# State-space branch of a two-layer encoder: tables multiplied in place from factors turned once, and a convolution kernel stored by rows and loaded shifted

## The chip, the core and the metric

One core of a Trainium2 chip runs the whole program: TensorE (PE in the profile, with its weight loads as PEld), VectorE (DVE), ScalarE (ACT), GpSimd (POOL), the SyncE queue (SP), which issues most transfers, and 16 DMA engines between device memory and the on-chip memory. The metric is the device time of one launch in microseconds; a kernel is run several times and the median is taken. Each profile is one further execution.

## The reference, cut to what matters

The input is 1024 tokens of 1024 channels. Layer 0 projects the normalised input to `u`, gates, `q`, `k` and `v`. Its branch A, around which this change lies, is a diagonal complex state space in 64 groups of 16 channels with 64 states each:

```
bu_re = einsum('tbgh,gnh->tbgn', u_c, bb_re)     # bb = coef * b, complex
x_t   = lb * x_(t-1) + bu_t                      # lb = mag * (cos + i sin), per group and state
y     = einsum(xr, cre) - einsum(xi, cim) + dsk * u
y     = gelu(y); y = y * sigmoid(y @ glu_w + glu_b) * silu(g_s5)
```

Branch B is an eight-head chunkwise retention. One output projection joins both; layer 1 is a gated causal convolution of width 31 with a norm; every layer adds its input, and a last norm follows. All is float32 in and out.

## The kernel before, in words

**Products.** Every large product is three TensorE passes on 128x512 tiles: operands are split into a rounded part and a rest, and `mm3` (L276 to L278) adds hi*hi, hi*lo and lo*hi. One block of 128 output channels is 2 halves of 8x3 matmuls, so 48 in all. Weights come in order through `wnext`, two blocks ahead: SP loads them (`wf`), ACT rounds them (`wh`, L267), DVE or POOL makes the rest (`wl`, L268).

**The front of layer 0.** Eight blocks `u0` to `u7` make `u`, which goes to device memory (`u_d`) in a layout of 8 taps of 128 steps. DVE computes the state-space constants meanwhile (`s5_params`): powers of the multiplier for 0 to 8 steps (`pr`, `pi`), unit phases in two levels (`e1`, `e2`), and the coefficients with which POOL makes `bbr`, `bbi` (L607). Then come 16 gate blocks `g8` to `g23` (`gate_block`). With each pair of them goes one block B of the state space, 128 channels (0 to 7):

- `s5_tables(B)`, on POOL: three complex outer products of small factors (`outer`, L790 to L792; two products and one sum for the real part, the same for the imaginary part, so 18 instructions of 128x512): `Mr`, `Mi` (input side), `Tc`, `Ts` (phases), `W3` (output side). They are chained in this order, one block after another.
- `s5_states(B)`: TensorE turns `Mr`, `Mi` (8 transposes of 128x128, L837; ACT copies them to `W2`), multiplies them with `U` (L848, banks `v`). DVE turns phases, scans over the steps (L863) and turns back (L856 to L875), which gives the states `S`. Then eight small matmuls `kp` (L882, L883) with `cbr`, `cbi`, block-diagonal copies of the output coefficients from the host, give the convolution kernel of 8 taps; DVE adds the skip term (L886), TensorE turns it (L888), it is stored to `k_d`, and one load (L895) brings it back shifted into `Wd`, which ACT sorts into `W1` (L897).
- `s5_out(B)`: `y` = `W1` times `U` (L912) plus `W3` times `S` (L918), 24 products in the rows of the order, copied by ACT to `yb` and stored to `y_d`.

Beside this DVE makes sums of inputs (`input_sums`) and of output weights (`weight_sums`, L249 to L252) for later use, loaded and made in the same gate block, except the input sums of two gate blocks, which are made one block later.

**What sets the order.** A scheduler orders each engine's instructions from the program's order, priorities and its own estimate of times; `chained` and `issue_after` add order by hand. On the chip each engine and each queue runs its list in order. Aux banks are five, product banks three. Weight tiles, tables and buffers rotate by tag, so a buffer's next writer waits for its last reader.

**After the front.** Value products and retention (`mm_v`, `ktp`, `ro`), the GLU (`mm_glu`), the output projection (`mm_w`), layer 1 (`mm_a`, `mm_b`, `mm_g`, the convolution on DVE and POOL, `mm_oc`) and the final norm follow. The change does not touch them.

Of the kernel before, what the change touches and what calls it, by code (L numbers as in the profile page):

```python
# [57 lines left out]
class Trunk:  # L58
# [179 lines left out]
    def weight_sums(self, pool, k):  # L238

        nb, c = k // 2, slice(k % 2 * HALF, (k % 2 + 1) * HALF)  # L240
        v, a = self.nc.vector, []
        for q, (r, tag) in enumerate(((0, "wa"), (4, "wb"), (12, "wc"), (8, "wd"))):
            a.append(pool.tile([P, HALF], F32, name=f"a{q}_{k}", tag=tag, bufs=2))
            self.nc.sync.dma_start(a[q][:], self.A["w_out"][r + nb].rearrange("p k n -> p (k n)")[:, c])
        a11, s3, s2, s4 = (t[:] for t in a)
# [50 lines left out]
    def run(self):  # L296
# [21 lines left out]
        self.k_d = dt("k_d", [8, 112 + P, P])  # L318
# [18 lines left out]
    def layer0_front(self, st):  # L337
# [100 lines left out]
        def u_block(nb):  # L438
            ut = uv.tile([P, 8, P], F32, name=f"ut_{nb}", tag="ut", bufs=2)

            def evac(h, ps):
# [3 lines left out]
                    r.rearrange("p (m j) -> p j m", j=8), op=ALU.mult)  # L445
            if nb < 2:
                for h in range(2):
                    evac(h, u01[nb][h])
            else:
                scaled(nb, self.wnext(f"u{nb}"), f"u{nb}", evac)  # L450
            nc.sync.dma_start(self.u_d[nb].rearrange("j h g m -> (h g) j m"), ut[:])

        def gate_block(nb, w, dst):
# [8 lines left out]
            nc.sync.dma_start(dst[k * P:(k + 1) * P], gt[:])  # L462
# [3 lines left out]
        with self.tc.issue_after(xdma.ins), self.tc.issue_after(r_diag.ins):  # L466
            zero = ev.tile([P, P], F32, name="zero")
            nc.gpsimd.memset(zero[:], 0.0)
            nc.sync.dma_start(self.k_d[:, :112].rearrange("b r c -> r b c"),
                              zero[:112].unsqueeze(1).broadcast_to([112, 8, P]))  # L470
            self.s5_params(sp, ev)
        u_block(3)
        u_block(4)
        early.close()
        sums = self.pool("sums", 1, stack=st)
        self.s5 = self.pool("s5w", 1, stack=st)
        for nb in range(5, 8):
            u_block(nb)
        self.s5_tab, self.s5_back, self.s5_last = {}, {}, None
        self.s5_tables(0)  # L480
        for nb in range(8, 24):
# [15 lines left out]
            with self.tc.issue_after(self.gate_evac.ins):  # L497
                if nb in (9, 11):
                    odd = self.input_sums(sums, nb - 9)
                elif nb in (10, 12):  # L500
                    self.input_sums_made(*self.input_sums(sums, nb - 9))
                elif 13 <= nb < 21:
                    self.weight_sums(sums, nb - 13)
# [82 lines left out]
    def s5_params(self, sp, tp):  # L586
# [31 lines left out]
        self.cbr, self.cbni = load("s5_cbr", (NP, 32)), load("s5_cbi", (NP, 32))  # L618
# [3 lines left out]
        v.tensor_scalar(self.cbni[:], self.cbni[:], -1.0, None, op0=ALU.mult)  # L622
# [95 lines left out]
        self.pr, self.pi = pr_, pi_  # L718

# [24 lines left out]
        grow(e2r, e2i, 7)  # L744
        self.e1 = (e1r, e1i)
# [24 lines left out]
        self.bbr, self.bbi = t((NP, 16), keep="s5_bbr"), t((NP, 16), keep="s5_bbi")  # L770
# [3 lines left out]
        gp = nc.gpsimd  # L774
        tt(x1[0], br[:], bc(cfr), ALU.mult, gp)
# [3 lines left out]
        tt(self.bbr[:], x1[0], x1[1], ALU.subtract, gp)  # L779
        tt(self.bbi[:], x1[2], x1[3], ALU.add, gp)  # L780
# [3 lines left out]

    def outer(self, B, o_r, o_i, ar, ai, br, bi, view, op_r=ALU.subtract, op_i=ALU.add):

        gp = self.nc.gpsimd
        for o, op, (a0, b0), (a1, b1) in ((o_r, op_r, (ar, br), (ai, bi)), (o_i, op_i, (ar, bi), (ai, br))):
            t = self.big(f"o_{B}", "tmpP", 2)
            yield gp.tensor_tensor(view(t[:]), a1, b1, op=ALU.mult)  # L790
            yield gp.tensor_tensor(view(o), a0, b0, op=ALU.mult)
# [980 lines left out]
```

## Time and profile before

| what | value |
|---|---|
| three runs | 1175.82, 1178.74, 1178.51 us; median 1178.51 |
| span of the profiled execution | 1173.9 us (the page gives no other time of this execution) |
| PE / PEld / DVE / ACT / POOL busy | 1161.3 / 965.5 / 910.5 / 545.1 / 713.5 us |
| mean granted TensorE clock | 0.999 |
| moved by DMA | 270.66 MB, mean 231 GB/s |
| one pair of gate blocks with one state-space block | 29.5 us, eight of them from 97 to 333 us |

The page divides the span into 40 slices with the busy share of each engine in tenths; the views by window, by line and by time give durations and what ended each wait. "Idle before" at an engine counts only where that engine sets the end. A matmul's record overlaps the next one's, so the distance between two starts, not the record's length, is what one costs.

### The profile page before, as it was taken

To read this page: it belongs to the slowest core of one execution; us is meant where nothing else is said; L and a number is where in the kernel's file an instruction comes from. 1 tells how busy PE (TensorE), PEld (TensorE's weight loads), DVE (VectorE), ACT (ScalarE), POOL (GpSimd) and SP (SyncE) were. 2 spreads that over 40 slices of the span, in tenths; PEclk is the share of its full clock that TensorE was granted. 3 is DMA by queue.
4 is the path that set the end of the run, shared out by engine and by line. 5 is a ranking of instruction groups with operands and counts; after the bars stand their busy time and mean duration, and the time that the engine had idled before them with its cause. 6 is when DMAs were issued, how large, how long until landed. Compare 5 with 4: busy or idle time off the path is not lost.

```text
span 1173.9 us, 17492 instructions
## 1 busy us (share of the span) xinstructions
PE 1161.3 (99%) x6150; PEld 965.5 (82%) x6150; DVE 910.5 (78%) x1507; ACT 545.1 (46%) x821; POOL 713.5 (61%) x507
## 2 busy tenths in 40 slices
PE   9999999999999999999999999999999999999997
PEld 7888888888888888887788888888888888888887
DVE  7875789999717475689777888479999999999643
ACT  7212343332226642123645544367756678544662
POOL 2049999888843245664444034348894689977742
PEclk9999999999999999999999999999999999999999
DMA  9353378778789765765988468965448553357863
GB/s 344 109 178 109 134 270 312 272 269 282 273 307 325 268 228 192 251 190 180 362 313 304 160 220 268 309 232 188 161 158 306 216 182 132 134 176 243 281 247 138
DMA packets 131192, 270.66 MB, mean 231 GB/s; under 512 B 12832, under 2 KB 41760, under 8 KB 130976
## 3 DMA queue, kind: packets, MB, share of 16 engines
q1 hardware_dynamic: 129952, 265.35, 66.5%
q10 hardware_dynamic: 1152, 4.19, 0.9%
q8 instruction: 48, 0.79, 0.3%
q14 instruction: 40, 0.33, 0.1%
HBM read 193.54 MB, written 71.76 MB: 226 GB/s over the span
## 4 chain that ended last, share of the span: by engine, by line
PE 91%; DMA 4%; DVE 2%; SPq 1%; ACT 1%; POOL 1%; issue 1%; DVEq 0%; POOLq 0%; ACTq 0%
PE mm_g L277 8%; PE mm_g L278 8%; PE mm_g L276 7%; PE mm_w L278 4%; PE mm_w L277 4%; PE mm_w L276 4%; PE mm_a L278 2%; PE mm_b L277 2%; PE mm_a L276 2%; PE mm_b L278 2%; PE mm_a L277 2%; PE mm_b L276 2%; PE mm_u L278 2%; PE mm_oc L278 2%; PE mm_u L277 2%; PE mm_oc L277 2%
## 5 line engine op out<-in xcount | busy, mean ns | idle before, releaser
L1461 DVE SCALAR_TENSOR_TENSOR cv<-u,convw,cv 128x512 f32<-128x512 f32 x358 | 244.7, 750 | 5.0 <-ACT cv L1447 3.5
L1441 POOL TENSOR_TENSOR tp<-tp,tp 128x512 f32<-128x512 f32 x104 | 138.9, 1338 | 28.7 <-ACT tp L1440 23.4
L278 PE MATMUL mm_g<-xh,wl_g 128*128 128x512 f32 x256 | 100.8, 394 | 0.0
L277 PE MATMUL mm_g<-xl,wh_g 128*128 128x512 f32 x256 | 100.7, 394 | 0.0
L276 PE MATMUL mm_g<-xh,wh_g 128*128 128x512 f32 x256 | 100.5, 393 | 0.0
L1440 ACT ACTIVATE tp<-u,convw 128x512 f32<-128x512 f32 x104 | 69.6, 713 | 9.6 <-POOL tp L1441 9.4
L277 PEld LDWEIGHTS mm_g<-xl,wh_g 128*128 128x128 f32 x256 | 48.1, 188 | 11.2 <-issue 1.6
L278 PEld LDWEIGHTS mm_g<-xh,wl_g 128*128 128x128 f32 x256 | 48.0, 188 | 10.5
L276 PEld LDWEIGHTS mm_g<-xh,wh_g 128*128 128x128 f32 x256 | 48.1, 188 | 9.6
L278 PE MATMUL mm_oc<-zh,wl_woc 128*128 128x512 f32 (+1 forms) x152 | 54.5, 360 | 0.2 <-DMA wl_woc<-lo_woc 0.2
L276 PE MATMUL mm_oc<-zh,wh_woc 128*128 128x512 f32 (+1 forms) x152 | 54.3, 362 | 0.0
L277 PE MATMUL mm_oc<-zl,wh_woc 128*128 128x512 f32 (+1 forms) x152 | 54.0, 357 | 0.0
L276 PE MATMUL mm_glu<-yh,wh_glu 128*128 128x512 f32 x128 | 50.0, 392 | 1.3 <-ACT sg L1250 1.3
L277 PE MATMUL mm_u<-xl,wh_u 128*128 128x512 f32 x128 | 50.1, 391 | 1.0 <-DVE xl L390 0.9
L276 PE MATMUL mm_g<-h1h,wh_cg 128*128 128x512 f32 x128 | 50.3, 393 | 0.0
L276 PE MATMUL mm_a<-h1h,wh_ca 128*128 128x512 f32 x128 | 50.3, 393 | 0.0
L278 PE MATMUL mm_b<-h1h,wl_cb 128*128 128x512 f32 x128 | 50.3, 393 | 0.0
L232 ACT CAST lh<-lf 128x512 fp32r<-128x512 f32 x32 | 19.5, 618 | 65.9 <-DMA lf<-w_c 59.3
L278 PE MATMUL mm_a<-h1h,wl_ca 128*128 128x512 f32 x128 | 50.0, 391 | 0.0
L277 PE MATMUL mm_glu<-yl,wh_glu 128*128 128x512 f32 x128 | 50.0, 392 | 0.0
L278 PE MATMUL mm_g<-h1h,wl_cg 128*128 128x512 f32 x128 | 49.9, 390 | 0.0
L277 PE MATMUL mm_g<-h1l,wh_cg 128*128 128x512 f32 x128 | 49.9, 390 | 0.0
(811 smaller groups left out, 3637.3 us busy)
## 6 DMA issues: line engine op xcount, KB each, us to landing
wf_g<-w_ab SPq DMA_DIRECT2D x16, 512.0 KB, 5.4
a<-w_out SPq DMA_DIRECT2D x32, 256.0 KB, 4.4
ws<-a SPq DMA_DIRECT2D x32, 256.0 KB, 4.8
lf<-w_c SPq DMA_DIRECT2D x32, 256.0 KB, 5.3
wf_p<-ws SPq DMA_DIRECT2D x16, 512.0 KB, 4.1
wf_cb<-w_c SPq DMA_DIRECT2D x16, 512.0 KB, 4.9
wf_ca<-w_c SPq DMA_DIRECT2D x16, 512.0 KB, 4.7
wl_cb<-lo_cb SPq DMA_DIRECT2D x16, 512.0 KB, 3.4
```

Of the source, the lines that this page charges most:

```text
L232: self.nc.scalar.copy(hi[:], f[:])
L276: nc.tensor.matmul(ps, wh[:, kb, :], xh, start=start, stop=False)
L277: nc.tensor.matmul(ps, wh[:, kb, :], xl, start=False, stop=False)
L278: self.last_mm = nc.tensor.matmul(ps, wl[:, kb, :], xh, start=False, stop=stop)
L1440: nc.scalar.mul(sk[:], u[:, k:k + HALF], cw[:, nb, k:k + 1])
L1441: gp.tensor_tensor(s0[:], s0[:], sk[:], op=ALU.add)
L1461: v.scalar_tensor_tensor(dst[:], *tap, accs_[i][:], op0=ALU.mult, op1=ALU.add)
```

## The change

- **Input tables.** The factors are turned once: after the first half of `u6`, TensorE transposes `pr`, `pi` (4) and `bbr`, `bbi` (8), ACT copies the three banks and stores them to device memory (`pt_d`, `bt_d`). For each block four loads (`PT`, `BT`, real and imaginary) bring the factors already repeated over rows, and POOL multiplies them in place (`outer`, 6 plain instructions of 128x512) into the turned table itself. The 8 transposes and 2 copies of each block are gone. Block 0's loads are on ACT's queue, the others on SP's, and these tables have one buffer each.
- **Phase and output tables.** `outer3` makes a complex product with three real products and two sums (5 instructions in place of 6) from precomputed sums (`psum`, `csum`, `cdif`, `e1s`, `e2s`, and `e1i - e1r` in place of `e1i`). A block thus has 16 POOL instructions in place of 18. `W3` has nine taps, of which the first is a copy of the output coefficients by ACT.
- **Convolution kernel.** `kp` is made from `W3` and block-diagonal copies of `bbr`, `bbi` made on the chip by ACT (the host's `cbr`, `cbi` and their two loads of 512 KB are gone); four small products with the identity add the skip term. The result is stored by rows of 112+128 and loaded by eight shifted loads straight into `W1`: the transpose, the DVE sum, the copy `Kt` and ACT's sorting copy are gone. The zeros of `k_d` are now 112 columns in place of 112 rows.
- **Times and queues.** `s5_kernel(B+1)` is called one gate block ahead of its states; `s5_states(B)` comes after the first gate block of its pair in place of before it. Input and weight sums are loaded one gate block before they are made. The stores of gates and of `y` move from SP's to ACT's queue. `U` is loaded with the tables. `R8`, `tmpP` and `tmpV` have fewer buffers.

The diff, cut:

```diff
@@ u_block
+                if (nb, h) == (6, 0):
+                    with tc.issue_after(self.last_mm.ins):
+                        self.s5_turned(ev)
@@ gate_block
-            nc.sync.dma_start(dst[k * P:(k + 1) * P], gt[:])
+            nc.scalar.dma_start(dst[k * P:(k + 1) * P], gt[:])
@@ layer0_front
         for nb in range(8, 24):
             B = (nb - 8) // 2
+            gate_block(nb, self.wnext(f"g{nb}"), self.gs_d if nb < 16 else self.gr_d)
             if nb % 2 == 0:
+                if B:
+                    self.s5_out(B - 1)
+                if B < 2:
+                    self.s5_kernel(B)
                 self.s5_states(B)
-                if nb in (10, 12):
-                    with self.tc.issue_after(self.last_kg.ins):
-                        self.input_sums_made(*odd)
-            gate_block(nb, self.wnext(f"g{nb}"), self.gs_d if nb < 16 else self.gr_d)
-            if nb % 2 == 0 and B:
-                self.s5_out(B - 1)
-            if nb % 2 and B < 7:
-                self.s5_tables(B + 1)
+                if B < 7:
+                    self.s5_tables(B + 1)
+            elif 0 < B < 7:
+                self.s5_kernel(B + 1)
...
+    def s5_turned(self, tp):
...
+            for i, src in enumerate(srcs):
+                nc.tensor.transpose(ps[:, i * P:(i + 1) * P], src, self.ident[:])
+            t = tp.tile([P, 8, P], F32, name=f"turned_{name}", tag="xin", bufs=8)[:, :4, :]
+            self.last_turn = nc.scalar.copy(t.rearrange("p i n -> p (i n)"), ps[:])
+            n = len(srcs) // len(dsts)
+            for i, dst in enumerate(dsts):
+                nc.scalar.dma_start(dst.rearrange("(i p) n -> p i n", p=P), t[:, i * n:(i + 1) * n, :])
...
+        for blk, b in zip(self.bblk, (self.bbr, self.bbi)):
+            for g in range(2):
+                r = slice(64 * g, 64 * g + 64)
+                with self.tc.issue_after(self.last_turn.ins):
+                    nc.scalar.copy(blk[r, :, 16 * g:16 * g + 16], b[r].rearrange("p h q -> p q h"))
...
+    def outer(self, B, ar, ai, br, bi):
+
         gp = self.nc.gpsimd
...
+        t = self.big(f"o_{B}", "tmpP", 1)
+        for o, a, b, op in ((t, ai, bi, ALU.mult), (ai, ai, br, ALU.mult), (br, ar, br, ALU.mult), (br, br, t, ALU.subtract),
+                            (ar, ar, bi, ALU.mult), (ar, ar, ai, ALU.add)):
+            yield gp.tensor_tensor(o[:], a[:], b[:], op=op)
+
+    def outer3(self, B, o_r, o_i, k1, k2, k3, view, op_i):
...
@@ s5_tables
+        queue = nc.sync if B else nc.scalar
+        self.chained(queue.dma_start(t[:], bass.AP(tensor=d.tensor, offset=d.offset + qs.start * P, ap=ap))
+                     for t, d, ap in zip((PT[0], BT[0], PT[1], BT[1]), (self.pt_d[0], self.bt_d[0], self.pt_d[1], self.bt_d[1]),
+                                         ([[32 * P, 8], [0, 16], [1, 4 * P]], [[0, 8], [32 * P, 16], [1, 4 * P]]) * 2))
...
+        order = (inputs, outputs, turns) if B == 0 else (outputs, inputs, turns) if B == 1 else (outputs, turns, inputs)
+        self.s5_last = self.chained(chain(*order), self.s5_last)
@@ s5_states
-            for q in range(4):
-                nc.tensor.transpose(ps[:, q * P:(q + 1) * P], M[:, q, :], self.ident[:])
-            t = self.big(f"W2{nm}_{B}", f"W2{nm}", 1)
-            nc.scalar.copy(t[:].rearrange("p q n -> p (q n)"), ps[:])
...
-        nc.tensor.transpose(kp[:, :P], Kg[:], self.ident[:])
...
+    def s5_kernel(self, B):
...
+        made += [nc.tensor.matmul(kp[r, :P], self.bblk[0][:, q0 + q, :], W3[:, 0, q, :P], start=True, stop=False)
+                 for q, r in enumerate(rows)]
+        made += [nc.tensor.matmul(kp[r, :16], self.ident[:, r], self.dd[:, B, :], start=False, stop=False) for r in rows]
+        made += [nc.tensor.matmul(kp[r, :P], self.bblk[1][:, q0 + q, :], W3[:, 1, q, :P], start=False, stop=True)
+                 for q, r in enumerate(rows)]
+        self.chained(made)
+        Kg = self.s5.tile([P, P], F32, name=f"Kg_{B}", tag="Kg", bufs=1)
+        copied = nc.scalar.copy(Kg[:], kp[:, :P])
+        nc.scalar.dma_start(self.k_d[B, :, 112:], Kg[:])
...
+        for g in range(8):
+            nc.sync.dma_start(W1[:, g, :], bass.AP(tensor=kd.tensor, offset=kd.offset + g * 16 * n,
+                                                   ap=[[16, 8], [n, 16], [1, P]]))
```

**TensorE around block 0.** Names: `mm_u7`, `mm_g8`, `mm_g9` are products of those blocks, `turn_*` the new transposes. Before, the transposes stand between `u7` and `g8`, and states and `kp` late in the first half of `g8`:

```order
L277 MATMUL mm_u7_1_1010<-xl_7_1_219,wh_u7_859 128x512
L278 MATMUL mm_u7_1_1010<-xh_7_1_218,wl_u7_860 128x512
L837 MATMUL w2r_0_1073<-ident_69,Mr_0_1037 128x128 x4
L837 MATMUL w2i_0_1080<-ident_69,Mi_0_1038 128x128 x4
L276 MATMUL mm_g8_0_1153<-xh_0_0_134,wh_g8_919 128x512
```

Now the twelve transposes stand in the middle of `u6`, and `kp` and the states of block 0 stand in the middle of the first half of `g9`, twelve matmuls after its start:

```order
L282 MATMUL mm_u6_0_927<-xh_7_0_214,wl_u6_803 128x512
L810 MATMUL turn_p_957<-ident_69,s5_pr_574 128x128 x2
L810 MATMUL turn_p_957<-ident_69,s5_pi_575 128x128 x2
L810 MATMUL turn_br_966<-ident_69,s5_bbr_728 128x128 x4
L810 MATMUL turn_bi_974<-ident_69,s5_bbi_729 128x128 x4
L280 MATMUL mm_u6_1_986<-xh_0_1_142,wh_u6_802 128x512
```

```order
L282 MATMUL mm_g9_0_1293<-xh_3_0_174,wl_g9_1023 128x512
L941 MATMUL kp_0_1176<-W3_0_1092,s5_bblkr_474 32x128 x4
L943 MATMUL kp_0_1176<-s5_s5_dd_478,ident_69 32x16 x4
L944 MATMUL kp_0_1176<-W3_0_1092,s5_bblki_475 32x128 x4
L903 MATMUL v0_0_1206<-U_0_1086,PTr_0_1082 64x128 x8
L903 MATMUL v1_0_1215<-U_0_1086,BTr_0_1084 64x128 x8
L280 MATMUL mm_g9_0_1293<-xh_4_0_184,wh_g9_1022 128x512
```

The states of block 0 have moved back by about one and a quarter gate blocks, and they no longer wait for transposes of their own. From block 2 on `kp` stands between the blocks of a pair and `y` and `v` side by side after the pair's first block.

**ScalarE's queue at the turned factors.** Nothing of this stood there before. `ptr`, `pti`, `btr`, `bti` are the tensors in device memory, `PTr_0` to `BTi_0` block 0's tables:

```order
L812 COPY turned_br_971<-turn_br_966 128x512
L815 DMA ptr_953<-turned_p_962 128x2x128
L815 DMA pti_954<-turned_p_962 128x2x128
L815 DMA btr_955<-turned_br_971 128x4x128
L812 COPY turned_bi_979<-turn_bi_974 128x512
L827 COPY s5_bblkr_474<-s5_bbr_728 64x32x16 x2
L827 COPY s5_bblki_475<-s5_bbi_729 64x32x16 x2
L815 DMA bti_956<-turned_bi_979 128x4x128
L871 DMA PTr_0_1082<-ptr_953 128x1x512
L271 CAST wh_g9_1022<-wf_g9_1021 128x1024
L871 DMA BTr_0_1084<-btr_955 128x1x512
L871 DMA PTi_0_1083<-pti_954 128x1x512
```

`BTi_0` comes next. The store of `bti` stands behind four copies, and the loads behind that store. **POOL's chain** continues from there; before, `Mr` followed `bbi` directly:

```order
L615 TENSOR_TENSOR s5_bbi_729<-s5bb1_731 128x32x16
L838 TENSOR_TENSOR o_0_1095<-BTi_0_1085,PTi_0_1083 128x512
L838 TENSOR_TENSOR BTi_0_1085<-BTi_0_1085,PTr_0_1082 128x512
L838 TENSOR_TENSOR PTr_0_1082<-BTr_0_1084,PTr_0_1082 128x512
L838 TENSOR_TENSOR PTr_0_1082<-PTr_0_1082,o_0_1095 128x512
L838 TENSOR_TENSOR BTr_0_1084<-BTr_0_1084,PTi_0_1083 128x512
L838 TENSOR_TENSOR BTr_0_1084<-BTr_0_1084,BTi_0_1085 128x512
L844 TENSOR_TENSOR o_0_1102<-s5_psum_610,s5_s5_cr_470 128x512
```

The first of these waits for the loads of `BTi_0` and `PTi_0`.

More of the change, by code (lines that the diff above doesn't have):

```diff
@@ L473, in layer0_front @@
         u_block(4)
+        for nb in (5, 6):
+            u_block(nb)
         early.close()
@@ L854, in s5_states @@
         vr, vi = V[0][:], V[1][:]
-        t2, t4 = (fl(self.big(f"m{i}_{B}", "tmpV", 4)) for i in range(2))
+        t2, t4 = (fl(self.big(f"m{i}_{B}", "tmpV", 2)) for i in range(2))
         v.tensor_tensor(t2, vi, ts, op=ALU.mult)
@@ L874, in s5_states @@
         v.tensor_tensor(c1(S[:, 0]), c0(zr), c0(t2), op=ALU.subtract)
-        v.tensor_tensor(c1(S[:, 1]), c0(zi), c0(t3), op=ALU.add)
+        self.last_s = v.tensor_tensor(c1(S[:, 1]), c0(zi), c0(t3), op=ALU.add)
         v.memset(S[:].rearrange("p c q m -> p (c q) m")[:, :, 0:1], 0.0)
-        kp = self.bank(f"kp_{B}")
-        for q in range(4):
-            o = kp[q * 32:(q + 1) * 32, :P]
-            nc.tensor.matmul(o, self.cbr[:, q0 + q, :], Mr[:, q, :], start=True, stop=False)
-            nc.tensor.matmul(o, self.cbni[:, q0 + q, :], Mi[:, q, :], start=False, stop=True)
@@ L894, in s5_states @@
-        kd = self.k_d[B]
-        nc.sync.dma_start(Wd[:], bass.AP(tensor=kd.tensor, offset=kd.offset, ap=[[P, P], [16 * P, 8], [1, P]]))
-        W1 = w.tile([P, 8, P], F32, name=f"W1_{B}", tag="W1", bufs=2)
-        nc.scalar.copy(W1[:].rearrange("p g (i h) -> p i g h", i=8), Wd[:].rearrange("p i (g h) -> p i g h", g=8))
-        self.s5_back[B] = U, W1, W3, S
+        self.s5_state[B] = S
+    def s5_kernel(self, B):
+        nc, W3 = self.nc, self.s5_tab[B][2]
+        q0 = 4 * B
+        kp, made = self.bank(f"kp_{B}"), []
+        rows = [slice(q * 32, (q + 1) * 32) for q in range(4)]
+        made += [nc.tensor.matmul(kp[r, :P], self.bblk[0][:, q0 + q, :], W3[:, 0, q, :P], start=True, stop=False)
[7 more added lines that the diff above has]
+        nc.scalar.dma_start(self.k_d[B, :, 112:], Kg[:])
+        R8 = self.s5_r8[B] = self.big(f"R8_{B}", "R8", 1)
+        with self.tc.issue_after(copied.ins):
+            for q in range(4):
+                nc.scalar.mul(R8[:, q, :], self.m01[:], self.r8[:, 4 * B + q:4 * B + q + 1])
+        W1 = self.s5.tile([P, 8, P], F32, name=f"W1_{B}", tag="W1", bufs=2)
+        kd, n = self.k_d[B], 112 + P
+        for g in range(8):
+            nc.sync.dma_start(W1[:, g, :], bass.AP(tensor=kd.tensor, offset=kd.offset + g * 16 * n,
+                                                   ap=[[16, 8], [n, 16], [1, P]]))
+        self.s5_w1[B] = W1
@@ L1739, in layout @@
     A["s5_cr"], A["s5_ci"] = c(inp["s5_c_re"][0]), c(inp["s5_c_im"][0])
-    for k in ("r", "i"):
-        cc = A["s5_c" + k].reshape(2, 64, 32, 16)
-        z = np.zeros((2, 64, 32, 2, 16), f)
-        for g in range(2):
-            z[g, :, :, g, :] = cc[g]
-        A["s5_cb" + k] = z.reshape(P, 32, 32)
     dd = np.zeros((8, 8, 16, 16), f)
```

124 lines of the change are left out of this document (68 added, 56 removed).

## The prediction

> **What bounds the kernel now.** I read the page's busy table and chain first, then what TensorE waited for, then the gate blocks by windows.
>
> ```profile
> span 1173.9 us, 17492 instructions
> PE 1161.3 (99%) x6150; PEld 965.5 (82%) x6150; DVE 910.5 (78%) x1507; ACT 545.1 (46%) x821; POOL 713.5 (61%) x507
> PE 91%; DMA 4%; DVE 2%; SPq 1%; ACT 1%; POOL 1%; issue 1%; DVEq 0%; POOLq 0%; ACTq 0%
> PE mm_glu L276 <- ACT sg L1250: 1.3, 1, 1.3
> PE mm_oc L278 <- DMA wl_woc<-lo_woc: 0.2, 1, 0.2
> ```
>
> The first three rows are the page's, the other two are the longest and the last wait of TensorE over the whole span: outside the head and the tail it is never idle for longer than 1.3 us. The chain follows it for 91%. So a pass taken from TensorE is worth its time, wherever it stands, as long as no other engine comes late; a pass added costs the same.
>
> ```profile
> 126.61:156.11 29.50, 29.50 (x203) 24.69 (x202) 24.14 (x29) 9.94 (x18) 27.68 (x20) 1.00 0.55 196
> 185.62:215.12 29.50, 29.50 (x203) 24.69 (x202) 28.14 (x32) 9.92 (x19) 27.33 (x20) 1.00 0.86 301
> 274.14:303.64 29.50, 29.50 (x203) 24.68 (x202) 27.36 (x30) 8.03 (x14) 25.74 (x19) 1.00 0.80 276
> ```
>
> These are windows of one pair of gate blocks each: length, then PE, PEld, DVE, ACT and POOL busy, granted clock, DMA share, GB/s. PE fills each window at full clock. But DVE (24.1 to 28.1) and POOL (25.7 to 27.7) are nearly full as well; the slack of the two is the second thing that decides.
>
> **The change part by part.** First TensorE's prices, from its instructions in order of time (start, length):
>
> ```profile
> 90.02 0.39 PE L276 MATMUL mm_u<-xh,wh_u 128*128 128x512 f32 x1
> 99.99 0.39 PE L278 MATMUL mm_u<-xh,wl_u 128*128 128x512 f32 x1
> 100.67 0.39 PE L278 MATMUL mm_u<-xh,wl_u 128*128 128x512 f32 x1
> 102.01 0.40 PE L277 MATMUL mm_g<-xl,wh_g 128*128 128x512 f32 x1
> 106.58 0.39 PE L276 MATMUL mm_g<-xh,wh_g 128*128 128x512 f32 x1
> 109.73 0.39 PE L278 MATMUL mm_g<-xh,wl_g 128*128 128x512 f32 x1
> 115.65 0.39 PE L277 MATMUL mm_g<-xl,wh_g 128*128 128x512 f32 x1
> 116.22 0.40 PE L276 MATMUL mm_g<-xh,wh_g 128*128 128x512 f32 x1
> ```
>
> From 90.02 to 99.99 there are 44 matmuls: 0.2266 us each. From 100.67 to 102.01 stand two steps of this and the 8 transposes: 1.34 - 0.45 = 0.88, so 0.11 a transpose. From 106.58 to 109.73 stand two steps, `v` and `kp`: 2.70. From 115.65 to 116.22 two steps and the transpose of `Kg`: 0.12. The merged chain gives the rest (start, time):
>
> ```profile
> 156.11 0.44 PE w2r L837 x4
> 156.55 0.44 PE w2i L837 x4
> 162.01 1.90 PE v L848 x32
> 171.19 1.79 PE y L912 x16
> 172.98 1.99 PE y L918 x32
> ```
>
> So `v` is 1.90, `y` 3.78, and `kp` with what it costs to turn aside is 2.70 - 1.90 = 0.80, in 16 passes on quarters of the array; without some 0.25 for the turn these are 0.55, or 0.034 a pass.
>
> *Removed*: 9 transposes in each of 8 blocks, 8 x (0.88 + 0.12) = 8.0 us. *Added once*: 12 transposes at 0.11 and one more turn aside of 0.1: 1.4. *Added per block*: four small products with the identity, 8 passes of 16 columns. No row has these. At `kp`'s price they are 8 x 0.034 = 0.27; at that of a full pass of `y` (1.79 / 16 = 0.112) 0.9; and the new order, which takes all four quarters one after another, may give `kp` back 0.1, so below nothing down to -0.1. I take 0.2, next to `kp`, since they stand on the same quarters: 1.6 for eight blocks, between -0.8 and 7.2. TensorE's sum is -8.0 + 1.4 + 1.6 = **-5.0**; a pair shrinks from 29.5 to some 28.7.
>
> The rest costs nothing if it stays hidden. Two groups of it by line:
>
> ```profile
> L897 ACT COPY W<-Wd 128x1024 f32<-128x1024 f32 x8 | 8.4, 1052 | 47.2 <-DMA Wd<-k_d 47.2
> L886 DVE TENSOR_TENSOR Kg<-Kg,s_s_dd 128x16 f32<-128x16 f32 x8 | 5.7, 714 | 0.0
> ```
>
> ACT, at 8 to 10 of 29.5 us a pair, gives up two copies of 0.58, `Kt` and the 1.05 of `W1`, and takes two small copies and store issues. DVE gives up 0.7 for the skip term: its 27.4 becomes 26.7 in 28.7. DMA moves four more loads of 256 KB a pair: 276 GB/s in 29.5 us is 8.1 MB, so 9.2 MB in 28.7, 320 GB/s, where 301 took a share of 0.86; so 0.91, full but not over. SP had 24 transfers in a pair and gets 31 (it loses `k_d`, `Wd`, `y_d`, two gate stores; it gains 4 + 8). Its loads for block B+1 wait for block B's `v`, because these tables have one buffer, and behind them wait loads of `w_out`, which DVE sums 16 us or more later; the weights behind them are two blocks (22 us) ahead. What is late in the states is DVE's, and `S` is needed by `y` a whole pair later than `v`.
>
> **The one place where it may show is the first blocks.** Block 0's tables used to follow `bbi` on POOL. Now they wait for a round trip.
>
> ```profile
> 38.80 0.69 DVE L622 TENSOR_SCALAR s_s_cbi<-s_s_cbi 128x1024 f32<-128x1024 f32 x1
> 67.95 0.44 DVE L607 TENSOR_TENSOR s_e1r<-s5t,s5t 128x256 f32<-128x256 f32 x1
> 81.64 1.29 POOL L607 TENSOR_TENSOR s_bbi<-s5bb 128x512 f32<-128x512 f32 x1
> L839 ACT COPY W2r<-w2r 128x512 f32<-128x512 f32 x8 | 4.6, 579 | 0.0
> L934 ACTq DMA_DIRECT2D yn_d<-yn x8: 326/362/389, 364.7 to 417.6; - x8
> xa<-xT SPq DMA_DIRECT2D x8, 256.0 KB, 5.3
> outT<-fo SPq DMA_DIRECT2D x8, 256.0 KB, 2.2
> x<-xT SPq DMA_DIRECT2D x7, 512.0 KB, 8.9
> ```
>
> DVE gets sums of 288, 544 and 544 columns ahead of the coefficients, by the 0.44 of 256 columns some 1.9, and loses 0.69: `bbi`, done at 82.9, is done near 84.1. TensorE reaches the middle of `u6` at 100.90 - 72 x 0.2266 = 84.6 and asks for `bbi` at 85.4: no wait, with 1.3 to spare. The banks are turned at 85.9. ACT then has, after two copies, three stores (0.36 each), a copy and four copies of half the lanes (0.58 each): the store of `bti` is issued near 90.9. It lands, and three issues later (1.1) the last load starts and lands. A transfer of 256 KB took 5.3 in just this stretch (the row of `xa`, windowed at 74 to 110 us), 2.2 in an empty one: POOL starts between 90.9 + 2.2 + 1.1 + 2.2 = 96.4 and 102.6. `U`, `u_d` and eight `xa` fill the queue here, so I take **100.5**, near the upper end.
>
> ```profile
> 108.00 1.11 POOL L790 TENSOR_TENSOR o<-s_bbi,s_pi 128x512 f32<-128x512 f32 x1
> 132.75 1.11 POOL L790 TENSOR_TENSOR o<-s_bbi,s_pi 128x512 f32<-128x512 f32 x1
> 160.46 2.09 POOL L790 TENSOR_TENSOR o<-s_bbi,s_pi 128x512 f32<-128x512 f32 x1
> ```
>
> These rows each start a block's 18 instructions: 24.75 us, or 1.375 an instruction, while DVE was lightly loaded, then 27.71, or 1.54. TensorE asks for `kp_0` at 100.90 + 1.4 + 60 x 0.2266 = 115.9, for which POOL must have made 11 instructions; for `kp_2` (37) at 115.9 + 2.8 + 84 x 0.2266 + 6.6 + 10.9 = 155.2; for `v_2` (48) at 155.2 + 0.9 + 10.9 + 3.8 = 170.8. POOL, with 22 at 1.375 and the others at 1.54, is there at 115.6, 153.9 and 170.8: just in time three times. Later it gains, 16 x 1.5 = 24 us of work in 28.7. So a start between 96.4 and 102.6 costs TensorE 0 to 2.1 us once; I take 0.7.
>
> ```profile
> 85.14 1.22 DVE L268 TENSOR_TENSOR wl_g<-wf_g,wh_g 128x1024 fp32r<-128x1024 f32 x1 [4.67 <-ACT wh_g L267]
> 85.26 2.26 POOL L792 TENSOR_TENSOR Mr<-Mr,o 128x512 f32<-128x512 f32 x1
> 89.73 1.30 POOL L792 TENSOR_TENSOR Mi<-Mi,o 128x512 f32<-128x512 f32 x1
> ```
>
> A POOL instruction that starts just behind a DVE one with two inputs lasts 2.26 instead of 1.30. The Trainium skill, page "SBUF — State Buffer", section "Who interferes with whom", says why: a VectorE instruction with two inputs in SBUF and a GpSimd one that reads SBUF exclude each other for their whole length. By that rule alone, POOL's instructions could never overlap DVE's sums and low halves, and the first blocks would pay those in full; the trace agrees in these three rows, and this is the first rival's mechanism.
>
> **The sum.** -5.0 + 0.7 = -4.3. The span would be 1169.6; the median of the runs shown stands 4.6 above the profiled span, which I take as what lies around it, so the forecast is 1178.5 - 4.3 = **1174.2**. That nothing behind the front gives it back follows from TensorE having no wait there that another engine's clock time sets; the 1.3 us at `mm_glu` hangs on products of retention, which move along.
>
> **The rivals.** *POOL paces the first blocks.* If the 1.54 holds from the start, `v_2` waits until 100.5 + 48 x 1.54 = 174.4, with the later start 176.5: a stall of 3.6 to 5.7, and the time is 1177.1 to 1179.2, no change. For it speak the two rows of 1.375 and 1.54 and the windows with POOL at 27.7; against it that DVE has nothing to do for block 0 until its tables are there. *The round trip is slow* (the slower side). The store of `bti` and the load behind it may take what loads took at the queue's fullest, 8.9 each: POOL starts at 90.9 + 8.9 + 1.1 + 8.9 = 109.8, 9.3 later, and all of it lands on TensorE at `kp_0` and `v_2`: 1178.5 - 5.0 + 9.3 = 1182.8. It makes the kernel slower than the uncertainty from a start at 109 on. Against it stands 5.3 as the landing time in this stretch. *The kernel does not give what it says*: if the identity products cost full passes, 7.2 instead of 1.6, TensorE gains nothing and the time is 1179.8 with the same 0.7. Against it stand `kp`'s 0.034. *DVE paces the pairs*: it decides only if DVE needs over 28.7 a pair, and its fullest window, 28.1 less 0.7, does not; at 30 us it would cost six pairs 1.3 each, 1182.
>
> ```profile
> k_d<-zero SPq DMA_DIRECT2D x1, 448.0 KB, 10.1
> ```
>
> One more rule speaks against a detail. The Trainium skill, page "DMA: Bandwidth & Descriptors", section "Specifications", gives 512 bytes as the smallest transfer at full rate; the zeros of `k_d` now go in rows of 448 bytes in the full queue of the head. By the rule that store lasts longer than its 10.1 us in the trace, and can hold up `x`; no row of before shows rows below 512 bytes by themselves.
>
> **How the numbers follow.** Chances: forecast 0.56, POOL pacing 0.17, slow round trip 0.12, full-price products 0.10, DVE 0.05. The forecast's own range, from the ends of its two unknown terms taken half way, is 1171 to 1177; the range over all takes in the first and third rival: 1171 to 1180.5. A measurement of this kernel can tell about 0.3%, 3.5 us, from no change. The forecast lies 4.3 below, only 0.8 beyond that bound, so of its 0.56 some 0.45 counts as faster, and the lower ends of the rivals add 0.08; slower are the slow round trip, DVE and a part of the full-price products: 0.15; the rest, 0.32, is no change.
>
> **What would show it.** Right: windows of a pair of 28.5 to 28.8 us from block 3 on with PE full; no transposes but twelve; TensorE idle once at most, under 2 us, before `kp_0`, `kp_2` or `v_2`, released by POOL. Wrong: a POOL instruction on `BTi` that starts after 103; waits of TensorE for POOL in several blocks or for banks held by DVE; the identity products longer than 0.4 us a block; pairs that do not shrink.

## The result, and the profile after

The changed kernel takes 1209.03 us (median of four runs, 1208.46 to 1212.94) against 1177.72 us before (four runs, 1175.82 to 1178.74): a ratio of 1.0276, 95% interval 1.0258 to 1.0295. It is slower by some 31 us. The forecast was 1174.2, the range ended at 1180.5, so both missed. One execution further down, of the kernel with only the order 16 x 8, ran at a mean granted clock of 0.556 and took 1946.37 us; its time is left out there, and the profile of that kernel is of this execution.

The profiled execution has a span of 1206.4 us, 32.5 more than before. The page, with the same rows that opened the prediction (span, busy time, shares of the chain by engine):

```profile
span 1206.4 us, 17642 instructions
PE 1166.9 (97%) x6154; PEld 967.5 (80%) x6154; DVE 906.4 (75%) x1502; ACT 534.9 (44%) x812; POOL 698.5 (58%) x495
PE 74%; DMA 13%; DVE 5%; POOL 4%; issue 2%; ACT 1%; SPq 1%; ACTq 0%; DVEq 0%; POOLq 0%
```

TensorE is still the busiest engine, but it holds 74% of the chain where it held 91, and transfers hold 13% where they held 4. What it waited for, the five longest over the whole span (total, times, longest):

```profile
PE v L903 <- POOL PTr L838: 10.3, 3, 7.2
PE v L903 <- POOL BTr L838: 8.4, 5, 2.4
PE kp L944 <- POOL W L848: 2.7, 2, 1.9
PE kp L941 <- POOL W L846: 1.8, 1, 1.8
PE mm_v L1123 <- ACT wh_V L166: 1.9, 1, 1.9
```

Before, no wait between the head and the tail was longer than 1.3 us. Now the products `v` and `kp` wait for POOL's tables, 23.2 us in all, and in most blocks, not once. POOL in turn waited for this, between 80 and 400 us:

```profile
POOL o L838 <- DMA BTi<-bti: 43.7, 6, 13.0
POOL o L838 <- DMA xa<-xT: 18.9, 1, 18.9
POOL o L838 <- DMA ws<-a: 9.9, 1, 9.9
```

`o` is the first product of a block's input tables, and it needs the loads of the turned factors. All eight of its waits end with a transfer (two are put down to other transfers that came last there, `xa` and `ws`): by this view POOL is not too slow, it has nothing to work on. Five of the pairs, from the start of one block's `y` to that of the next (length, then PE, PEld, DVE, ACT, POOL busy, granted clock, DMA share, GB/s):

```profile
174.86:204.92 30.06, 29.14 (x202) 23.97 (x201) 26.86 (x32) 7.67 (x17) 20.81 (x14) 1.00 0.89 286
204.92:245.96 41.04, 32.48 (x201) 26.65 (x200) 24.55 (x29) 7.12 (x16) 28.01 (x21) 0.83 0.82 273
245.96:274.48 28.52, 28.52 (x201) 23.84 (x200) 23.20 (x29) 7.12 (x16) 18.20 (x13) 1.00 0.89 290
274.48:308.89 34.41, 30.30 (x202) 25.03 (x200) 23.78 (x29) 7.13 (x16) 23.95 (x18) 0.95 0.82 271
308.89:341.60 32.71, 30.32 (x201) 24.96 (x200) 20.60 (x24) 7.13 (x16) 22.80 (x17) 0.95 0.80 258
```

One pair has no wait: 28.52 us with PE full, where a pair took 29.50. So TensorE's saving is there, 0.98 a pair. The other four give it back many times over: 1.5, 12.5, 5.9 and 4.2 us above 28.52. About two thirds of that is waiting; most of the rest is the clock, as the lowered means of the granted clock in three of the rows show. TensorE's instructions around the longest wait (start, length):

```profile
216.05 1.98 PE L903 MATMUL v<-U,PTr 128*64 128x128 f32 x16 [7.20 <-POOL PTr L838]
219.39 1.97 PE L903 MATMUL v<-U,BTr 128*64 128x128 f32 x16 [1.37 <-POOL BTr L838]
222.31 0.63 PE L282 MATMUL mm_g<-xh,wl_g 128*128 128x512 f32 x1
222.74 0.63 PE L280 MATMUL mm_g<-xh,wh_g 128*128 128x512 f32 x1
225.59 0.39 PE L281 MATMUL mm_g<-xl,wh_g 128*128 128x512 f32 x1
225.82 0.40 PE L282 MATMUL mm_g<-xh,wl_g 128*128 128x512 f32 x1
```

After 8.6 us of waiting the matmuls start 0.43 us apart until 225.3 and then again 0.23: windows of one microsecond there show a granted clock of 0.50. The pair's 12.5 us are 8.6 of wait and some 4 of half clock.

The loop that this forms is seen whole at block 7. Block 6's `v` is over at 317.3. SP's queue, what the loads stand behind, and the loads (start, length of the issue):

```profile
319.49 0.48 SPq L874 DMA_DIRECT2D U<-u_d  x1
320.71 1.43 SPq L258 DMA_DIRECT2D ws<-a  x2
324.46 0.84 SPq L258 DMA_DIRECT2D ws<-a  x1
325.41 0.60 SPq L871 DMA_DIRECT2D PTr<-ptr  x1
328.28 0.57 SPq L871 DMA_DIRECT2D BTi<-bti  x1
```

and POOL's first and last instruction on them, and TensorE's second half of `v`:

```profile
339.22 1.29 POOL L838 TENSOR_TENSOR o<-BTi,PTi 128x512 f32<-128x512 f32 x1 [9.20 <-DMA BTi<-bti]
348.06 1.26 POOL L838 TENSOR_TENSOR BTr<-BTr,BTi 128x512 f32<-128x512 f32 x1
349.38 1.09 PE L903 MATMUL v<-U,BTr 128*64 128x128 f32 x16 [1.47 <-POOL BTr L838]
```

From `v` to the first load's issue 8.1 us, to the last issue 2.9, to its landing 10.9, POOL's six instructions 10.1: 32 us from `v` to `v`, against 28.52 of work for TensorE.

### The profile page after: what moved, and what is told of

It is laid out like the page before. It is cut to its first block, busy times and chain, and to the rows that moved or that the text cites. A ratio compares the mean times of both kernels' runs of the same rounds, so it can differ in the third digit from the quotient of the medians.

```text
span 1206.4 us, 17642 instructions
## 1 busy us (share of the span) xinstructions
PE 1166.9 (97%) x6154; PEld 967.5 (80%) x6154; DVE 906.4 (75%) x1502; ACT 534.9 (44%) x812; POOL 698.5 (58%) x495
## 4 chain that ended last, share of the span: by engine, by line
PE 74%; DMA 13%; DVE 5%; POOL 4%; issue 2%; ACT 1%; SPq 1%; ACTq 0%; DVEq 0%; POOLq 0%
PE mm_g L280 5%; PE mm_g L281 4%; PE mm_g L282 4%; PE mm_w L280 4%; PE mm_w L282 4%; PE mm_w L281 4%; PE mm_oc L280 2%; PE mm_oc L282 2%; PE mm_a L282 2%; PE mm_oc L281 2%; PE mm_b L282 2%; PE mm_b L281 2%; PE mm_a L280 2%; PE mm_a L281 2%; PE mm_b L280 2%; PE mm_glu L280 2%
## 5 line engine op out<-in xcount | busy, mean ns | idle before, releaser
L280 PE MATMUL mm_g<-xh,wh_g 128*128 128x512 f32 x256 | 103.3, 403 | 0.0
L1501 ACT ACTIVATE tp<-u,convw 128x512 f32<-128x512 f32 x104 | 69.7, 714 | 11.1 <-POOL tp L1502 10.9
L466 ACT ACTIVATE gt<-gt 128x512 f32<-128x512 f32 x32 | 20.2, 632 | 107.0 <-DVE gt L465 78.8
L465 DVE TENSOR_TENSOR gt<-mm_g,R 128x512 f32<-128x512 f32 x32 | 21.8, 684 | 43.4 <-PE mm_g L282 43.4
L838 POOL TENSOR_TENSOR o<-BTi,PTi 128x512 f32<-128x512 f32 x8 | 10.3, 1284 | 72.4 <-DMA BTi<-bti 43.7
```

The lines of the kernel that those rows point to most:

```text
L280: nc.tensor.matmul(ps, wh[:, kb, :], xh, start=start, stop=False)
L465: self.gate_evac = nc.vector.tensor_tensor(gt[:, c], ps[:], self.R[:, c], op=ALU.mult)
L466: nc.scalar.activation(gt[:, c], gt[:, c], AF.Silu)
L838: yield gp.tensor_tensor(o[:], a[:], b[:], op=op)
L1501: nc.scalar.mul(sk[:], u[:, k:k + HALF], cw[:, nb, k:k + 1])
```

## The experiments

All ratios are to the kernel before on the same chip. Where no interval is given, a kernel was run once. The kernels that were run several times spread over up to 10 us when their loads come late (1182.67 to 1192.32 for one below), so a few us between two single runs say nothing.

### Leave the loads out

```diff
+        if B == 0:
+            self.s5_pt, self.s5_bt = (... one set of four tables ...)
+        PT, BT = self.s5_pt, self.s5_bt
+        if B == 0:
             self.chained(queue.dma_start(t[:], ...) ...)
```

> The changed kernel without the four loads of the turned factors for blocks 1 to 7: POOL multiplies again what block 0 left in the same four tables, so the state inputs of these blocks are left out (wrong numbers, same instructions on TensorE, DVE, ACT and POOL). Theory A (a loop through one buffer: states of block B-1 free the tables, the loads come 6 to 11 us later in SP's queue, land 11 to 13 us after their issue, POOL needs 8 to 10 us, then states of block B; 32 us and more against 28.5 us of TensorE work a pair): TensorE's waits for POOL before the states of blocks 3 and 5 to 7 (8.6 and 9.2 us) go, with the slow clock behind them; the wait of block 0 (3.7 us) stays; 1178 to 1184 us, pairs of 28.5 us. Theory B (POOL's own rate beside DVE, 16 instructions at 1.6 to 2.1 us): the waits stay within 30%, over 1195 us.

This kernel leaves out the state inputs of blocks 1 to 7. It takes 1176.88 us, against 1178.13 before. All waits for input tables were gone; what was left were the two at block 0's `kp`, 4.1 us together:

```profile
PE kp L944 <- POOL W L846: 2.2, 1, 2.2
PE kp L947 <- POOL W L848: 1.9, 1, 1.9
```

Theory B (POOL too slow beside DVE) falls: POOL does the same instructions here. The cause is with the loads. The time lies 1.1 us below the range, in a single run.

### Two buffers, and block 0's order

```diff
-        PT, BT = ([self.big(f"{n}{c}_{B}", n + c, 1) for c in "ri"] for n in ("PT", "BT"))
+        PT, BT = ([self.big(f"{n}{c}_{B}", n + c, 2 if c == "r" else 1) for c in "ri"] for n in ("PT", "BT"))
```

> The changed kernel with two buffers for the two tables that the states read (real parts), so that no load of block B+1 waits for the states of block B, and the loads stand up to a pair earlier in SP's queue; the same bytes are moved. Theory A (the loop through one buffer): as without the loads, 1178 to 1186 us, POOL's wait for the loads under 10 us in blocks 2 to 7 together. Theory B (POOL's rate): over 1195 us. Theory C (the transfers are too many: 1 MB more a pair in queues that are full): still over 1195 us, with POOL waiting for the loads as before (44 us), while the kernel without these loads is fast.

```diff
-        order = (inputs, outputs, turns) if B == 0 else (outputs, inputs, turns) if B == 1 else ...
+        order = (outputs, inputs, turns) if B == 1 else (outputs, turns, inputs)
```

> The changed kernel with one edit: block 0's output and phase tables are made ahead of its input tables, so POOL works on them while the round trip through device memory runs. Only the first stall is touched. Theory A: the wait of 3.7 us before kp and states of block 0 and its slow clock (some 2 us) go, the waits of blocks 3 to 7 stay: 1202 to 1206 us. If the later waits only take up what the first one leaves (they are set by a fixed point in time, as transfers in a full queue would be): 1207 to 1211 us.

> Both edits together: two buffers for the real tables, and block 0's output and phase tables first. Theory A: TensorE has no wait over 1 us in the gate blocks, and the sum of the prediction stands alone: 8 pairs 0.98 us shorter, 1.4 us of transposes, so 1177.7 - 6.5 = 1171 to 1176 us. Theories B and C: over 1190 us.

Two buffers: 1206.22 us, ratio 1.0237 (1.0222 to 1.0252). Block 0's order: 1205.04, 1.0235 (1.0218 to 1.0252). Both: 1196.36, 1.0156 (1.0141 to 1.0171). Theory A in its plain form (1178 to 1186 with two buffers, 1171 to 1176 with both) falls with the first and the third. The buffers did take away the waits of `v` for POOL, but the time did not go with them. What TensorE waited for with two buffers:

```profile
PE mm_v L1123 <- ACT wh_V L166: 12.6, 1, 12.6
PE kp L941 <- POOL W L846: 5.2, 1, 5.2
PE mm_g L280 <- DVE gt L465: 3.2, 3, 2.5
```

The same lateness comes out elsewhere, the largest piece 12.6 us behind the front, at the value products, whose weights ScalarE rounds late (`wh_V`). That speaks for the loop through one buffer as the place where the lateness showed and not as its source; the next kernel tests it. The order of block 0 is worth some 4 us by itself, as expected, and 10 on top of two buffers (1206.2 to 1196.4).

### The same loads from plain rows

```diff
+        if B:
+            src = [self.A["w_out"][2 * B + i // 2] ... 128 rows of 512 columns ... for i in range(4)]
+        self.chained(queue.dma_start(t[:], s) for t, s in zip((PT[0], BT[0], PT[1], BT[1]), src))
```

> The changed kernel with the four table loads of blocks 1 to 7 on the same queue, at the same places and of the same size, but from 128 different rows of a weight tensor in place of 8 or 16 rows repeated (so the state inputs of these blocks are left out: wrong numbers). Theory C1 (loads that repeat rows of device memory are slow in themselves; in a quiet stretch 1 MB of them and 0.5 MB of kernel rows kept the transfer engines only 0.45 busy): under 1190 us, with POOL's waits for the loads at half (44 to some 20 us) and landings near 5 us. Theory C2 (it is the loads' place and number: SP's list in order, the bytes in a full stretch, the one buffer): 1200 to 1212 us, as the change.

1185.69 us, again without the state inputs of blocks 1 to 7. Same queue, same places, same bytes, one buffer, block 0's order as in the change: some 23 of the 31 us are gone. POOL's waits for these loads were halved:

```profile
POOL o L838 <- DMA BTi<-w_out: 23.1, 6, 6.9
```

So it is neither the bytes nor the place alone: a load of the turned factors is slow in itself. That is C1, within its numbers for the time and for POOL's waits. The kernel changes three things of a load at once: its groups, the repetition, and the tensor that it reads (`w_out` in place of `pt_d` and `bt_d`, which the kernel itself writes).

### What makes such a load slow

The loads of the change read 8 groups of 16 rows, of which only 8 or 16 differ. Two kernels part the grouping from the repetition:

```diff
+        src: ... w_out ...          ap=[[P * D, 8], [D, 16], [1, 4 * P]]   # 8 groups of 16 different rows
+        src: ... pt_d and bt_d ...  ap=[[0, P], [1, 4 * P]]                # one row, 128 times
```

> The changed kernel with the table loads of blocks 1 to 7 from 128 different rows of a weight tensor, but written as 8 groups of 16 rows, as the loads of the change are (state inputs of these blocks left out). It parts two readings of the 1185.7 us of the kernel with plain rows. If a load slows because rows are repeated: as with plain rows, 1183 to 1189 us, two loads back to back in the quiet stretch after block 0's states at 340 to 360 GB/s. If it slows because its outer dimension is 8, so that only half of the transfer engines take part: 1203 to 1212 us, and in that stretch at most 185 GB/s with the engines 0.45 to 0.5 busy, as in the change.

> The other corner: the table loads of blocks 1 to 7 all read one row 128 times, as one group of 128 (state inputs of these blocks are wrong). If repeating rows is what slows: 1203 to 1215 us. If the outer dimension of 8 does: 1183 to 1189 us, and the rate of the two loads in the quiet stretch at 300 GB/s or above.

8 groups of different rows: 1199.18 us, between the two ranges. One row 128 times: 1209.99. Both leave out the state inputs of blocks 1 to 7. Neither reading was right alone: by these single runs each of the two costs. After block 0's states two table loads, 0.5 MB, are for some us the only transfers under way, but for the end of the loads of `W` before them. Windows of one microsecond there (the last two columns are the share of the transfer engines and GB/s), the change first:

```profile
133.00:134.00 1.00, 1.00 (x6) 0.84 (x5) 1.00 (x2) 0.22 (x1) 0.92 (x2) 1.00 0.50 184
134.00:135.00 1.00, 1.00 (x6) 0.81 (x6) 1.00 (x1) 0.84 (x1) 0.61 (x1) 1.00 0.32 119
135.00:136.00 1.00, 1.00 (x6) 0.84 (x5) 0.96 (x3) 0.00 (x0) 0.00 (x0) 1.00 0.49 170
```

then plain rows:

```profile
134.00:135.00 1.00, 1.00 (x7) 0.81 (x6) 1.00 (x2) 0.05 (x1) 0.77 (x1) 1.00 0.85 257
135.00:136.00 1.00, 1.00 (x6) 0.84 (x5) 0.96 (x3) 1.00 (x1) 0.00 (x0) 1.00 0.71 266
```

then 8 groups of different rows:

```profile
136.00:137.00 1.00, 1.00 (x6) 0.84 (x5) 1.00 (x3) 0.00 (x0) 0.00 (x0) 1.00 0.49 182
137.00:138.00 1.00, 1.00 (x6) 0.84 (x5) 1.00 (x3) 0.00 (x0) 0.00 (x0) 1.00 0.51 158
```

and one row 128 times:

```profile
135.00:136.00 1.00, 1.00 (x6) 0.84 (x5) 0.96 (x2) 0.81 (x1) 0.22 (x1) 1.00 0.65 162
136.00:137.00 1.00, 1.00 (x6) 0.84 (x5) 1.00 (x3) 0.25 (x1) 0.00 (x0) 1.00 0.88 152
```

The two windows of plain rows hold 523 KB, which is both loads: 2 us. The change needs more than 3 for the same bytes. With 8 groups, different rows or not, the share is never above 0.51 and the rate never above 184 GB/s, as if the load used half of the engines. With one row 128 times the engines are busier, and the rate in the windows shown is 152 and 162 all the same: reading a row again and again is slow in another way. Plain rows reach 257 and 266 in the same place.

The two kernels with repeated rows read tensors that the kernel writes itself, the two with different rows read `w_out`. That this is not the difference shows far behind, in the profile of the change: two loads of 256 KB with 128 different rows, `gl` and `x1l`, come from such tensors with nothing else under way, and 522 KB are moved in 2 us:

```profile
1082.00:1083.00 1.00, 1.00 (x6) 0.81 (x6) 1.00 (x3) 0.00 (x0) 0.00 (x0) 1.00 0.80 303
1083.00:1084.00 1.00, 1.00 (x6) 0.84 (x5) 1.00 (x3) 0.85 (x1) 0.44 (x1) 1.00 0.57 219
```

### The order 16 x 8

The tables' 128 rows are 8 taps x 16 channels. Putting them as 16 channels x 8 taps, with `U` and the shifted loads to match, gives all these loads 16 groups; the repetition stays.

```diff
-  [[32 * P, 8], [0, 16], [1, 4 * P]], [[0, 8], [32 * P, 16], [1, 4 * P]]
+  [[0, 16], [32 * P, 8], [1, 4 * P]], [[32 * P, 16], [0, 8], [1, 4 * P]]
-  self.u_d[B].rearrange("j h g m -> (j h) g m")
+  self.u_d[B].rearrange("j h g m -> h j (g m)")
-  ap=[[16, 8], [n, 16], [1, P]]
+  ap=[[n, 16], [16, 8], [1, P]]
```

> The changed kernel, with the 128 rows of the tables in the order 16 channels x 8 taps in place of 8 taps x 16 channels, in three access patterns (the table loads, the load of U, the eight shifted loads of the convolution kernel): the same values, bytes and number of transfers, and each of these loads now has an outer dimension of 16. The rows are still repeated. If the outer dimension of 8 is a main part of the cause in the change itself: two table loads in the quiet stretch after block 0's states at 300 GB/s or more, POOL's waits for the loads cut to half, and the time 1185 to 1197 us. If only repeating rows counts: 1205 to 1212 us.

> The same, with block 0's output and phase tables ahead of its input tables. By the same reading the first stall goes too: 4 to 6 us below the kernel with the order 16 x 8 alone; 1180 to 1192 us.

> The same as the one before, with two buffers for the real tables (loads on SP's queue). If what is left after the order 16 x 8 is the loop through one buffer: 1174 to 1180 us. If it is the transfers: within 3 us of the kernel with one buffer.

Alone 1207.96 us (1204.56 to 1208.61), ratio 1.0241 (1.0219 to 1.0264); with block 0's order 1199.55, 1.0182 (1.0155 to 1.0209); with two buffers as well 1193.58, 1.0123 (1.0100 to 1.0147). All three lie above the ranges in which the 8 groups, or the one buffer after them, would be a main part of the cause. The grouping by itself buys nothing: the kernel with 16 groups of repeated rows is where the change is. Its windows with the two table loads alone, 516 KB in 3 us:

```profile
202.00:203.00 1.00, 1.00 (x4) 0.50 (x3) 0.96 (x2) 0.00 (x0) 0.00 (x0) 0.56 0.52 176
203.00:204.00 1.00, 1.00 (x4) 0.61 (x3) 1.00 (x3) 0.00 (x0) 0.00 (x0) 0.56 0.56 176
204.00:205.00 1.00, 1.00 (x4) 0.50 (x3) 0.95 (x2) 0.00 (x0) 0.00 (x0) 0.56 0.54 164
```

The share is a little above a half, and the rate, 164 to 176, is no higher than with 8 groups: it seems that now the repetition sets it. The two limits are close, 184 GB/s at most for 8 groups and 152 to 176 for repeated rows, and lifting one of them leaves the other. Beside other edits the order does buy something: 5.5 us with block 0's order (1199.55 against 1205.04) and 6.1 with the loads on ScalarE's queue (below), in both cases with intervals of the ratio that do not touch.

### The loads on ScalarE's queue

> Two buffers for the real tables, block 0's other tables first, and all table loads on ScalarE's queue in place of SP's; the same bytes. If the loads' place in SP's list is the cause (they come 6 to 12 us behind the time at which their tables are free, and what stands behind them waits for their issue): TensorE's waits of this kernel with the loads on SP (9.1 us before the value products, 6.2 us before kp, 2.0 for DVE) shrink to a third and the time is 1174 to 1182 us. If it is the transfers themselves (bytes, repeated rows): 1190 to 1200 us, as with the loads on SP (1196).

> The kernel with two buffers, block 0's other tables first and the table loads on ScalarE's queue (1188.6 us), with plain rows in place of the repeated ones (state inputs of blocks 1 to 7 left out). If nothing is left but the rate of the loads: within 3 us of the kernel without loads and with the same order (1173.8), so 1173 to 1177 us. If their bytes cost as well, through the value weights that come late: 1180 to 1188 us.

> Order 16 x 8, two buffers, block 0's other tables first, and the table loads on ScalarE's queue: the kernel of 1188.6 us with all its loads spread over twice the engines. With plain rows it took 1176.8. If the rate of the loads was all that kept it above: 1174 to 1180 us, faster than or equal to before; if repeating rows costs by itself: 1182 to 1188 us.

> The kernel of 1182.5 us (order 16 x 8, two buffers, block 0's other tables first, table loads on ScalarE's queue) with one more edit: the loads of y for its pass through gelu go on ScalarE's queue too. Its one long wait of TensorE, 10.9 us before the value products, hangs on ScalarE's gelu, which waits for that load behind the value phase's loads in SP's list. If that place in the list is the cause: the wait shrinks to under 2 us and the time is 1169 to 1175 us, below the kernel before. If the transfers of this stretch are simply too many: the wait moves to the next load, 1179 to 1185 us.

With two buffers, block 0's order and the table loads moved by `queue = nc.scalar`: 1188.60 us, 1.0089 (1.0061 to 1.0117). That is 8 us below the same kernel with the loads on SP (1196.36), outside both ranges that I gave: the place in SP's list counts, but it is not all. With plain rows in addition, which leaves out the state inputs of blocks 1 to 7: 1176.79. With the order 16 x 8: 1182.51, 1.0041 (1.0026 to 1.0057), the fastest version with all its loads. TensorE's waits in its gate blocks are gone but for one of 1.6 us for DVE; what is left stands at the value products:

```profile
PE mm_v L1123 <- ACT wh_V L166: 10.9, 1, 10.9
```

I took that for a place in SP's list and moved the loads of `y` to ScalarE's queue (`nc.sync` to `nc.scalar` in `y_pass`). It was wrong: 1185.76, 1.0067 (1.0045 to 1.0089), and the wait is still 9.1 us. The profiles show what stands ahead of the late rounding in ScalarE's list: casts of `xf` and a gelu of `yp`. In the version at 1182.51 ScalarE waits 19.7 us for the first `xf`, until 365.3, and the gelu then follows `yp` at 373.1; after the move the gelu waits 8.8 us for `yp`, issued at 355.5, until 367.9. Why these loads come late is not shown. With plain rows the wait for `wh_V` was 0.6, so they seem late through what the slow loads leave behind.

### Old input tables in the new kernel, and no loads at all

```diff
+        M, W2 = W2, []
+        for nm, m in zip("ri", M):
+            for q in range(4):
+                nc.tensor.transpose(ps[:, q * P:(q + 1) * P], m[:, q, :], self.ident[:])
```

> The changed kernel with the input tables made as before: POOL multiplies the unturned factors, TensorE turns both tables of each block (8 transposes, 0.88 us a block), ACT copies them; the twelve transposes, the stores and the loads of the turned factors are gone. The convolution kernel by rows, the new order, the queues and the earlier loads of sums stay. If the loads of the turned factors are the whole cause: no stall, TensorE's work is the new pair of 28.5 plus 0.88, so 29.4, against 29.5: 1174 to 1179 us, no difference from before. If the rest of the change costs too: over 1182 us.

> Without the loads for blocks 1 to 7 (state inputs of these blocks left out, as in the first of these kernels) and with block 0's other tables first. If the prediction's sum for TensorE is right by itself, both stalls being gone: the 1176.9 us of the kernel without loads less the 4.1 us that TensorE waited there before kp and the 1 to 2 us of slow clock behind it: 1170 to 1173 us. If something else in the change costs (the eight shifted loads, stores on ScalarE's queue): 1175 to 1179 us.

> The kernel without the loads of blocks 1 to 7 and with block 0's other tables first (state inputs of these blocks left out), timed in rounds this time: what TensorE's sum is worth with no stall. One look gave 1173.8 us against 1178.2, so a ratio of 0.9963; if TensorE's sum of the prediction holds (-5.0 us), 1172 to 1175 us and the ratio's interval below 0.998.

Old input tables, everything else new: 1180.30 us, ratio 1.0014 (1.0001 to 1.0026), some 2 us above before and just above the range, with pairs of 29.58 us (`y` starts at 201.41 and 230.99). So the kernel by rows, the queues and the earlier loads of sums cost 2 or 3 us at most. Without the loads of blocks 1 to 7, and so without their state inputs, and with block 0's order: 1173.82 in a single run, and 1171.16 as the median of five (1170.55 to 1178.73), ratio 0.9942 (0.9926 to 0.9959). Two pairs of the single run:

```profile
137.92:166.44 28.52, 28.52 (x223) 23.75 (x222) 25.73 (x29) 11.35 (x24) 25.02 (x17) 1.00 0.78 257
166.44:194.96 28.52, 28.52 (x202) 23.84 (x201) 27.91 (x32) 7.00 (x15) 23.75 (x17) 1.00 0.87 295
```

That is TensorE's saving with nothing late: 6 to 7 us. It is what the change could have been worth if these loads had cost nothing. No version that keeps all its loads is below the kernel before.

## Why the prediction was wrong

- **TensorE's sum, -5.0.** Right in kind and a little small. 8 pairs x 0.98 = 7.8, less 1.4 for the twelve transposes and 0.5 for a wait at `turn_bi`, is -5.9; the kernel without the loads has -6.0 by its medians. The four products with the identity were the term that was furthest off: `kp` with them runs from 148.56 to 149.20 in the change, 0.64 where `kp` with its turn aside was priced at 0.80, and a pair is shorter by 0.98 where the nine transposes were priced at 1.00: so next to nothing instead of 0.2 a block. The third rival (full price) is out.
- **"DMA moves four more loads of 256 KB a pair ... full but not over."** This is the step that failed. I priced 1 MB as 1 MB. The rows quoted for 256 KB (2.2 empty, 5.3 in the head) are of transfers with 128 different rows, and the 2.2 is a store (`outT`); the new ones repeat 8 or 16 rows in 8 groups, and no row of before showed such a load. It had to be bounded like an operation the trace does not show, and it was not. By the runs it is worth some 23 us of the 31 (1209.0 against 1185.7 with plain rows). The forecast of 320 GB/s at a share of 0.91 did not come: the pairs shown moved 258 to 290 GB/s at 0.80 to 0.89.
- **A rule that spoke against it.** The Trainium skill, page "DMA: Bandwidth & Descriptors", section "Rules for kernel authors", says that the slowest dimension larger than one sets how many of the 16 transfer engines a transfer uses, and that "a leading zero-stride broadcast of c copies" keeps it on at most c of them. The prediction cited this page for the 512 bytes and passed over that. The trace agrees: a share of no more than 0.51 with 8 groups, 0.71 to 0.85 with 128 rows. By the rule alone the order 16 x 8 would have mended it, and it did not (1208.0): with repeated rows, of which that section says nothing, the rate stayed at 164 to 176 GB/s.
- **"Its loads for block B+1 wait for block B's `v`."** Said, and then not followed round: I asked what stands behind these loads in the queue, not when they land. From `v` on, 6 to 11 us in SP's list, some 3 of issue, 9 to 13 of landing and 8.5 to 10 of POOL until the next `v`: 32 us for block 7, against a pair of 28.5. POOL was taken as a rate ("it gains, 16 x 1.5 = 24 us of work in 28.7") when it was a link in a loop.
- **The first round trip, +0.7.** Right mechanism, mis-sized. The store of `bti` was issued at 89.2 (forecast 90.9), the last load at 94.2, but POOL started at 105.7, past my upper end of 102.6: 11.5 us from issue to start for that load, against 2.2 to 5.3. `kp` and `v` of block 0 waited 3.7 us, and half clock added some 2; the order of tables that avoids it is worth 4 us in its run (1205.0).
- **"TensorE idle once at most, under 2 us."** Wrong in size, and it hid a price: a wait of several us is followed by a stretch at half clock. In the three pairs with a lowered clock that is some 4, 1.8 and 1.8 us (the pair's length less 28.52 less its waits). The Trainium skill, page "TensorE: Matmul & The Clock Gate", section "Part 1: The HAM clock gate", has the array at half rate after about 3.4 us of idle window; the trace agrees with half (0.43 us a matmul against 0.23), but waits of 1.8 to 2.4 us, one or two of them within some us, were enough here, while 1.3 and 1.5 us at block 7 were not (the step there is 0.23).
- **The rivals.** POOL's pace decided nothing: with the loads out, the same 16 instructions were in time. The slow round trip had the right sign and place, and its condition came near (a start at 105.7, where 109 made it slower); but it was one event of 9 us, not one in each block. DVE did not pace the pairs. None of the four gives a time above 1182.8. The signs that it named for being wrong did come: a POOL instruction on `BTi` that starts after 103, and waits of TensorE for POOL in several blocks.
- **A smaller slip.** The 4.6 us between the profiled span and a run's time mix two executions; in one execution the two lie some 2 us apart (1206.4 and 1208.47 after). The forecast, 1178.5 less 4.3, does not hang on it.

What stays open: why repeated reads of the same rows are slow, what groups and repetition each cost (the kernels that part them were run once), and why the loads ahead of the value products come late in the best version.

## What to carry to other kernels

A transfer is priced by its access pattern, not its bytes: how many groups it has at the outside and whether it reads the same rows again; if the trace has no load of that form, bound it as an unknown. Where a buffer's reader releases a load that feeds the next reader, add the loop up, with the queue's list and the landing, against the period. Taking one link away (a buffer, a place in the list) moves a wait; check where it went before calling it the cause.

## What the runs showed of the hardware that was not expected

- In the quiet stretch loads of 256 KB in 8 groups of rows ran at no more than 184 GB/s with the engines at most 0.51 busy; with 128 plain rows at 257 to 266.
- Reading one row of device memory 128 times ran at 152 to 162 GB/s in two windows there, with the engines up to 0.88 busy, and the kernel was as slow as the change (1210.0 against 1209.0 us). 16 groups of repeated rows ran at 164 to 176.
- In the quiet stretch SP needed 0.57 to 0.60 us to issue a table load in 8 groups, and 0.43 to 0.46 for the same bytes as 128 plain rows or as one row 128 times.
